# Splitting the scan's products by weight columns, half of the array each

## The chip, the cores and the metric

The kernel runs on one core of one Trainium2 chip. Its time is the device time of one execution in microseconds, and smaller is better. The core has a matrix engine (TensorE, PE in the profile, its weight loads PEld), a vector engine (VectorE, DVE), an activation engine (ScalarE, ACT), a general engine (GpSimd, POOL) and a queue that issues most transfers (SyncE, SP). Each reads its own list of instructions in order, and they wait for one another by semaphores. TensorE takes a stationary operand (the weights, loaded ahead), streams a moving operand past it, and writes the product to PSUM, where the other engines read it. The stationary operand's columns become the product's partitions.

## The reference

One layer of a bidirectional mixer on 128 context tokens and 2048 latent tokens, all in f32, with 1024 channels. The normalised and modulated input goes through one wide projection. Half of the channels are eight heads of 64 with a delta-rule recurrence, run once per direction; the other half is a short gated convolution. An output projection and a last norm follow. What the change touches is the recurrence:

```python
def step(S, inp):
    r_t, w_t, k_t, v_t, kk_t, a_t = inp
    s_kk = jnp.einsum('bdhij,bdhj->bdhi', S, kk_t)
    S = (S * w_t[..., None, :] - s_kk[..., :, None] * (kk_t * a_t)[..., None, :]
         + v_t[..., :, None] * k_t[..., None, :])
    return S, jnp.einsum('bdhij,bdhj->bdhi', S, r_t)
s_final, ys = lax.scan(step, s0.astype(f32), xs)
```

The latent scans start from cached states (`state_wkv`), the context scans from zero, and the context's final states are an output too.

## The kernel before, in words

**Phase 1** makes the projections in blocks of 384 tokens and stores the scan's operands to memory. Its products (mm..., lines 158 to 160) use the whole array. Line 188 (`mod_rows`) makes the modulation rows: weights of 32 columns, each put on another strip of 32 of the array's columns (`ps[q:q + 32, :]`).

**Phase 2** is the scan. Tokens are cut into chunks of 64. Within a chunk the recurrence is solved with matrices, so that one product takes a chunk's state to the next. The work is cut into 17 stages: each takes one pair of heads in both directions (`gi` 0 and 1) and eight chunks of each; one stage is the context's. The stages overlap. While stage s is scanned, the following ones are prepared:

- `partM` (stage s+3): psF and psG (line 829, masked by VectorE at 830) and transposes psQ (822).
- `partI` (stage s+3): GpSimd inverts small triangular matrices (lines 851 to 872, tiles ab and zt), stores the inverse, and `partW` loads it again as zc (line 896).
- `partU`, `partB` (stage s+1): psU and psW (lines 910 and 917, tiles of 32x32 of the array, two at a time on different tiles), psX (936) and psE (947). VectorE masks psE into E (line 948).
- `partS` (stage s): the scan. For a chunk, direction and head, line 987 multiplies E, 128 rows by 128 columns, as the weights, by sv, 128 rows by 64 columns. sv holds the state in its upper 64 rows and the chunk's values in its lower 64. Of the product psS, the upper 64 partitions are the next state, the lower 64 the chunk's outputs.

Line 1000 (VectorE) scales the upper half by pc into the next chunk's sv, on which that direction's next product waits. After four chunks `outputs` copies or adds the lower half to y (lines 716 and 1017). Where a new pair of heads begins, its start state comes in by line 979 (in_st) and VectorE takes its mean off in lines 981 to 983.

**Phase 3**, the output projection (lines 1219 to 1221, psa and psu), fills in towards the end of the scan and goes on after it.

What sets the order: the generators above are woven by small tables (`ORDER`, `MORD`), and then the framework schedules each engine's instructions by its own estimate of times. So an edit to one line can move instructions on all engines, SP's loads among them. SP and GpSimd issue transfers strictly in their order; a load that waits holds those behind it.

Of the kernel before, what the change touches and what calls it, by code (L numbers as in the profile page):

```python
# [627 lines left out]
def phase2(K):  # L628
    nc, tc, A, S = K.nc, K.tc, K.A, K.S
    V, G, P, T = nc.vector, nc.gpsimd, nc.scalar, nc.tensor  # L630
# [102 lines left out]
    def tl(shape, tag, b, pool=None, dt=F32):  # L733
        return (pool or O.l0).tile(shape, dt, tag=tag, name=f"{tag}_{K.u()}", bufs=b)
# [29 lines left out]
    H0, H1, FULL = slice(0, 64), slice(64, 128), slice(0, 128)  # L764
# [187 lines left out]
    def partS(s, st, nxt):  # L952

        sp = {}
        for i in range(8):
            for gi, g in enumerate(st.g):
                d = g.d
                ctx = g.blk is None
                u = i % 4 * 2 + i // 4 if ctx else i
                u = u if d == 0 else 7 - u  # L960
                p, c = g.units[u]
                if ctx:
                    first = c == (0 if d == 0 else 1)
                    lastc = not first
                else:
                    first = c == (2 if d == 0 else 33)
                    lastc = c == (33 if d == 0 else 2)
                sv = g.sv
                n, k = (u // 4 if d == 0 else 1 - u // 4), u % 4

                m, q = (u % 2, u // 2) if ctx else (u // 4, u % 4)
                if i == 0 and not ctx and gi in held:
                    G.tensor_copy(sv[0:64, u], held.pop(gi)[:])
                if first:
                    if ctx:
                        G.memset(sv[0:64, u], 0.0)
                    else:
                        x = sv[0:64, u]
                        D(x, A["st0"][:, d, 2 * p:2 * p + 2, :])
                        mn = tl([64, 2], "mn", 2)  # L980
                        V.tensor_reduce(mn[:], x, mybir.AxisListType.X, ALU.add)
                        V.tensor_scalar(mn[:], mn[:], -1.0 / 64, None, ALU.mult)
                        V.tensor_tensor(x, x, mn[:].unsqueeze(2).broadcast_to((64, 2, 64)), ALU.add)
                if i % 4 == 0:
                    sp[gi] = O.pS.tile([128, 4, 2, 64], F32, tag="S", name=f"psS{s}_{gi}_{i}")
                for hd in range(2):
                    T.matmul(sp[gi][:, q, hd, :], g.E[n][:, k, hd, :], sv[:, u, hd, :], start=True, stop=True)  # L987
                if not (lastc and not ctx):
                    if ctx and lastc:
                        so = tl([64, 2, 64], "so", 2)  # L990
                        dst = so[:]
                    elif (not ctx) and i == 7:
                        if nxt.g[gi].blk is None:
                            held[gi] = tl([64, 2, 64], "held", 2)
                            dst = held[gi][:]
                        else:
                            dst = nxt.g[gi].sv[0:64, 0 if d == 0 else 7]
                    else:
                        dst = sv[0:64, u + (1 if d == 0 else -1)]
                    r = V.tensor_tensor(dst, sp[gi][0:64, q], B.pc[0:64, d, 2 * p:2 * p + 2, c:c + 1].broadcast_to((64, 2, 64)), ALU.mult)  # L1000
                    O.scaled = r.ins
                    if ctx and lastc:
                        D(S["nst"][:, d, 2 * p:2 * p + 2, :], so[:])
                if i % 4 == 3:
                    outputs(g.units[0][0], g.blk, m, sp[gi])
            yield

    def outputs(p, blk, m, ps):

        y, there = ynew.setdefault((p, blk), (None, []))  # L1010
        if y is None:
            y = tl([128, 4, 128], "y", 5)
            ynew[p, blk] = y, there
        r = slice(m * 64, m * 64 + 64)
        src = ps[64:128].rearrange("p q h v -> p q (h v)")
        if m in there:
            V.tensor_tensor(y[r], src, y[r], ALU.add)  # L1017
        else:
            copy("o", y[r], src)
        there.append(m)  # L1020
        if len(there) == 4:
            ynew.pop((p, blk))
            pend.append(finish(p, blk, y))
# [67 lines left out]
    def main():  # L1091
# [12 lines left out]
        for s in range(NST):  # L1104
# [30 lines left out]
            for i, _ in enumerate(partS(s, st, sts.get(s + 1))):  # L1135
                for _ in range((2, 2, 2, 1, 1, 0, 0, 0)[i]):
                    next(m, None)
                next(tail, None)
                if s < NST - 1:
                    emit(i + 1)  # L1140
                for f in todo[:1] if s < NST - 3 else todo:
                    next(f, None)
# [203 lines left out]
```

## Time and profile before

| what | value |
|---|---|
| three runs | 1759.25, 1768.68, 1767.44 us, median 1767.44 |
| profiled execution, span from first to last instruction | 1770.7 us |
| TensorE busy | 1649.1 us, 93% of the span |
| VectorE, ScalarE, GpSimd busy | 65%, 47%, 34% |
| mean granted TensorE clock | 0.968 |
| psS (line 987) | 1088 instructions, from 1045.2 to 1605.2 us |

The profiled execution has no time of its own beside its span; the page gives the span only. A row of a group reads: line, engine, operation, written tile <- read tiles, shape, count, then busy time in all and mean of one in ns, then the engine's idle time just before and what ended it. A row of the order of time reads: start in us, length in us, engine, line, operation, tiles, shape, count of merged instructions, and in brackets a wait before it. Lengths of TensorE instructions overlap the next one, since they are pipelined; so what an instruction takes is read from one start to the next. A product in f32 shows as two instructions. A row of waits reads: engine, line that waited, what it waited for, us in all, times, longest.

### The profile page before, as it was taken

The page shows a single profiled execution, that of the slowest core. Times are in us where ns is not written, and L with a number is a line of the kernel's source. Part 1 is how long each engine was busy: PE and PEld are TensorE (multiplying, and loading weights), DVE is VectorE, ACT ScalarE, POOL GpSimd, SP SyncE. Part 2 cuts the span into 40 slices and gives each one's busy share as a digit, 9 for nine tenths or more (in the row PEclk, how much of TensorE's full clock was granted, in tenths as well). Part 3 has the DMA queues.
Part 4 walks back from the last instruction along what each step waited for, and adds up shares of the span by engine and source line. Part 5 has one row for each costly group of instructions (what it writes and reads, how often), then busy time and mean ns, then how long its engine had stood idle before and what let it go on. Part 6 is the DMA issues. An engine that isn't in the chain of part 4 may idle for free. (4 is left out here: it accounts for less than half of the span.)

```text
span 1770.7 us, 33010 instructions
## 1 busy us (share of the span) xinstructions
PE 1649.1 (93%) x12400; PEld 1557.3 (88%) x12400; DVE 1157.2 (65%) x2197; ACT 831.2 (47%) x1607; POOL 601.3 (34%) x1089
## 2 busy tenths in 40 slices
PE   5999899999899999999999999899899899899998
PEld 3898899899888999999999989899799899787786
DVE  5998897545777635478843466777677677556333
ACT  4565544224454312255522177667567576433222
POOL 0132210001122100022205528877767868223221
PEclk9999999999899999999999989999899899899999
DMA  9788786564788743478776376767667784645432
GB/s 363 218 244 241 231 253 244 200 237 127 167 193 184 207 153 128 152 191 218 243 249 209 127 178 170 167 178 193 158 172 197 166 193 115 177 149 192 155 129 104
DMA packets 315376, 335.16 MB, mean 189 GB/s; under 512 B 166920, under 2 KB 263560, under 8 KB 301136
## 3 DMA queue, kind: packets, MB, share of 16 engines
q1 hardware_dynamic: 242912, 323.99, 61.5%
q10 hardware_dynamic: 70944, 4.60, 3.0%
q0 software_dynamic: 1360, 4.46, 0.7%
q8 instruction: 98, 1.61, 0.4%
q14 instruction: 62, 0.51, 0.1%
HBM read 221.16 MB, written 111.82 MB: 188 GB/s over the span
## 5 line engine op out<-in xcount | busy, mean ns | idle before, releaser
L871 POOL TENSOR_TENSOR zt<-zt,ztmp 128x30 f32<-128x30 f32 (+7 forms) x510 | 201.9, 396 | 39.7
L987 PE MATMUL psS<-sv,E 128*128 128x64 f32 x1088 | 153.1, 273 | 2.7 <-DVE sv L1000 2.5
L947 PE MATMUL psE<-str,stl 128*128 128x128 f32 x1088 | 149.3, 283 | 5.6 <-ACT str L714 3.8
L987 PEld LDWEIGHTS psS<-sv,E 128*128 128x128 f32 x1088 | 143.3, 197 | 5.9 <-DVE sv L1000 4.3
L947 PEld LDWEIGHTS psE<-str,stl 128*128 128x128 f32 x1088 | 135.0, 196 | 6.9 <-ACT str L714 4.6
L868 POOL TENSOR_TENSOR ztmp<-ab,zt 128x60 f32<-128x60 f32 (+7 forms) x255 | 132.4, 519 | 19.4
L716 ACT COPY bd<-rr 64x512 f32<-64x512 f32 x136 | 83.9, 617 | 90.2 <-issue 35.1
L314 POOL TENSOR_TENSOR shk<-rawl 128x384 f32<-128x384 f32 (+1 forms) x24 | 20.1, 838 | 277.1 <-ACT rawl L310 271.3
L948 DVE TENSOR_TENSOR E<-psE,msk 128x512 f32<-128x512 f32 x136 | 93.4, 687 | 24.3 <-PE psE L947 22.2
L936 PE MATMUL psX<-F,zb 128*128 128x128 f32 x544 | 79.6, 299 | 18.4 <-DVE E L948 13.2
L1000 DVE TENSOR_TENSOR sv<-psS,pc 64x128 f32<-64x128 f32 x254 | 67.9, 277 | 37.3 <-PE psS L987 35.6
L936 PEld LDWEIGHTS psX<-F,zb 128*128 128x128 f32 x544 | 71.8, 209 | 21.7 <-DVE E L948 16.1
L158 PE MATMUL mmv<-h,w 128*128 128x384 f32 (+1 forms) x192 | 70.1, 365 | 19.2 <-ACT q1r L312 10.1
L1282 POOL TENSOR_TENSOR z<-z,x 128x512 f32<-128x512 f32 x32 | 43.7, 1367 | 129.0 <-DVE z L1278 106.8
L829 PE MATMUL psF<-rr,bd 128*128 128x128 f32 x544 | 79.7, 294 | 2.7 <-ACT bd L716 1.8
L829 PE MATMUL psG<-rr,bd 128*128 128x128 f32 x544 | 74.7, 283 | 4.8 <-DVE F L830 4.8
L829 PEld LDWEIGHTS psF<-rr,bd 128*128 128x128 f32 x544 | 71.8, 206 | 3.3 <-issue 2.9
L829 PEld LDWEIGHTS psG<-rr,bd 128*128 128x128 f32 x544 | 68.3, 198 | 5.1 <-DVE F L830 5.0
L195 POOL TENSOR_TENSOR hsls<-sq,hshs 128x384 fp32r<-128x384 f32 (+1 forms) x24 | 31.6, 1318 | 109.5 <-DMA scr_vt<-vt 36.5
L159 PE MATMUL mmv<-h,w 128*128 128x384 f32 (+1 forms) x192 | 68.5, 357 | 0.0
L160 PE MATMUL mmv<-h,w 128*128 128x384 f32 (+1 forms) x192 | 68.0, 354 | 0.1
L158 PE MATMUL mmg<-h,w 128*128 128x384 f32 (+1 forms) x192 | 63.4, 330 | 4.0 <-ACT ta L374 2.0
(308 smaller groups left out, 5193.2 us busy)
## 6 DMA issues: line engine op xcount, KB each, us to landing
w<-scr_wsp SPq DMA_DIRECT2D x68, 1024.0 KB, 6.6
scr_wsp<-w SPq DMA_DIRECT2D x34, 1024.0 KB, 5.6
rr<-scr_ops SPq DMA_DIRECT2D x64, 512.0 KB, 5.0
scr_ops<-sp SPq DMA_DIRECT2D x160, 192.0 KB, 5.1
wr<-in_win SPq DMA_DIRECT2D x34, 512.0 KB, 7.5
ab<-scr_at SPq DMA_DIRECT2D x34, 256.0 KB, 3.8
x<-in_x SPq DMA_DIRECT2D x17, 512.0 KB, 3.7
wadas<-in_wada SPq DMA_DIRECT2D x8, 1024.0 KB, 15.2
```

What stands on the lines that cost most here:

```text
L158: T.matmul(ps[:, :n], w[:, 0, k], hh[:, 0, k, :n], start=k == 0, stop=False)
L159: T.matmul(ps[:, :n], w[:, 0, k], hh[:, 1, k, :n], start=False, stop=False)
L160: T.matmul(ps[:, :n], w[:, 1, k], hh[:, 0, k, :n], start=False, stop=k == 7)
L716: (V.tensor_copy if k in ON_DVE else P.copy)(dst, src)
L829: T.matmul(ps[:, i, :].rearrange("p (a b) -> p a b", b=64), w[:, u, :], x[:, :, u, :], start=True, stop=True)
L868: G.tensor_tensor(tv, ab[:, j:j + 2, j + 2:32].unsqueeze(1).broadcast_to((128, kn, 2, n)), zt[:, :kn, j:j + 2].unsqueeze(3).broadcast_to(( ...
L871: G.tensor_tensor(zt[:, :kn, j + 2:32], zt[:, :kn, j + 2:32], tv[:, :, r], ALU.subtract)
L936: T.matmul(px[:, i, :], B.zb[:, gi, us.start + i, :], g.F[:, us.start + i, :], start=True, stop=True)
L947: T.matmul(pe[:, i, hd, :].rearrange("p (b t) -> p b t", b=2), g.lt[:, :, hd, us.start + k + i].rearrange("p b t -> p (b t)"), g.rt[:, :, ...
L948: V.tensor_tensor(g.E[n][:, k:k + 2].rearrange("p a b c -> p (a b) c"), pe[:].rearrange("p a b c -> p (a b) c"), B.msk[:, ME[g.d]].unsquee ...
L987: T.matmul(sp[gi][:, q, hd, :], g.E[n][:, k, hd, :], sv[:, u, hd, :], start=True, stop=True)
L1000: r = V.tensor_tensor(dst, sp[gi][0:64, q], B.pc[0:64, d, 2 * p:2 * p + 2, c:c + 1].broadcast_to((64, 2, 64)), ALU.mult)
```

## The change

The product of a chunk and a head is issued as two: the first with E's first 64 columns as the weights, which writes psS's upper 64 partitions (the next state), the second with E's last 64 columns, which writes the lower 64 (the outputs). Both move the same sv. H0 and H1 are the slices 0 to 64 and 64 to 128. What is computed is the same.

```diff
                 for hd in range(2):
-                    T.matmul(sp[gi][:, q, hd, :], g.E[n][:, k, hd, :], sv[:, u, hd, :], start=True, stop=True)
+                    for r in (H0, H1):
+                        T.matmul(sp[gi][r, q, hd, :], g.E[n][:, k, hd, r], sv[:, u, hd, :], start=True, stop=True)
```

Lines below 987 move down by one: what is line 1000 above is 1001 in the changed kernel, and the products are in its line 988.

The schedule changes with it. In the rows below psS_0 and psS_1 are the two directions, and the number behind x counts products or pieces. TensorE in the second half of a stage of the scan, before:

```order
L947 MATMUL psE_0_10_11520<-str_10008,stl_10002 128x128 x4
L829 MATMUL psF_1_1_11635<-rr_8836,bd_8831 128x128 x3
L987 MATMUL psS_0_0_11558<-sv_11104,E_11366 128x64 x2
L829 MATMUL psF_1_1_11635<-rr_8836,bd_8831 128x128
L829 MATMUL psG_1_0_11641<-rr_8836,bd_8832 128x128 x3
L947 MATMUL psE_1_10_11526<-str_10009,stl_10003 128x128 x4
L987 MATMUL psS_1_0_11562<-sv_11113,E_11374 128x64
L947 MATMUL psE_0_11_11532<-str_10008,stl_10002 128x128 x4
L987 MATMUL psS_1_0_11562<-sv_11113,E_11374 128x64
```

and the same place now:

```order
L947 MATMUL psE_0_10_11616<-str_10008,stl_10002 128x128 x4
L829 MATMUL psF_1_1_11743<-rr_8836,bd_8831 128x128 x2
L988 MATMUL psS_0_0_11654<-sv_11168,E_11454 64x64 x4
L829 MATMUL psF_1_1_11743<-rr_8836,bd_8831 128x128 x2
L829 MATMUL psG_1_0_11749<-rr_8836,bd_8832 128x128 x2
L988 MATMUL psS_1_0_11660<-sv_11177,E_11462 64x64
L947 MATMUL psE_1_10_11622<-str_10009,stl_10003 128x128 x4
L988 MATMUL psS_1_0_11660<-sv_11177,E_11462 64x64
L947 MATMUL psE_0_11_11628<-str_10008,stl_10002 128x128 x4
L988 MATMUL psS_1_0_11660<-sv_11177,E_11462 64x64 x2
```

Steps of four pieces stand alone between products on the full array, and some steps are cut into runs of one or two pieces, as single products were before. Elsewhere the steps of both directions follow directly on one another, eight pieces in a row:

```order
L988 MATMUL psS_0_4_10588<-sv_10024,E_10332 64x64 x4
L988 MATMUL psS_1_4_10594<-sv_10033,E_10340 64x64 x4
L917 MATMUL psW_10549<-zc_10329,bu 32x32 x32
L988 MATMUL psS_0_4_10588<-sv_10024,E_10332 64x64 x4
L988 MATMUL psS_1_4_10594<-sv_10033,E_10340 64x64 x4
L829 MATMUL psF_0_1_10838<-rr_8835,bd_8831 128x128 x4
L988 MATMUL psS_0_4_10588<-sv_10024,E_10332 64x64 x4
L988 MATMUL psS_1_4_10594<-sv_10033,E_10340 64x64 x4
L936 MATMUL psX_0_0_10617<-F_8825,zb 128x128 x4
```

psW stands between two such runs. In the whole changed order the 1088 pieces stand in 240 unbroken runs: 24 of one piece, 13 of two, 11 of three, 128 of four, 7 of five, 1 of six, 2 of seven, 52 of eight, 1 of ten and 1 of twelve. From the first psS to the last the full array is left for narrower pieces 216 times (205 for psS, 11 for psU or psW), where before it was left 47 times, for psU and psW. 35 times a run of psS comes directly behind psU or psW, and 28 times one of those directly behind psS.

SP's queue also changed. At the stage that begins the third pair of heads (sv's new tiles are loaded here, with the values from scr_vt and the start state from in_st; ab and zc belong to GpSimd's inverses), before:

```order
L851 DMA ab_13060<-scr_at 64x1024 x2
L1074 DMA scr_mixT<-yo_12978 128x512
L896 DMA zc_13137<-scr_zt 64x16x32 x2
L1038 DMA sg_13234<-scr_sg 128x512
L759 DMA sv_13126<-scr_vt 64x8x128
L979 DMA sv_13126<-in_st 64x128
L759 DMA sv_13135<-scr_vt 64x8x128
L1038 DMA w_13330<-scr_q 128x512
L979 DMA sv_13135<-in_st 64x128
L805 DMA rr_8835<-scr_ops_57 128x2x512
```

and now:

```order
L979 DMA sv_13350<-in_st 64x128
L896 DMA zc_13361<-scr_zt 64x16x32
L759 DMA sv_13359<-scr_vt 64x8x128
L896 DMA zc_13361<-scr_zt 64x16x32
L1039 DMA w_13566<-scr_q 128x512
L805 DMA rr_8835<-scr_ops_57 128x2x512
L783 DMA stl_10002<-scr_ops_57 64x4x64 x2
L780 DMA str_10008<-scr_ops_57 64x2x256
L780 DMA str_10009<-scr_ops_59 64x2x256
L783 DMA stl_10003<-scr_ops_59 64x4x64 x2
L805 DMA rr_8835<-scr_ops_57 128x2x512
L979 DMA sv_13359<-in_st 64x128
```

The first direction's start state now stands ahead of zc, and the second direction's further behind it, beyond the loads of the next block. At the stage that begins the fourth pair the two moved in the same way; at the second pair, where one start state stood ahead of zc, both now do.

## The prediction

> **What bounds the kernel now.** I read the page's first part, then a table of stretches, then who TensorE waited for, then the order of time around the scan.
>
> ```profile
> PE 1649.1 (93%) x12400; PEld 1557.3 (88%) x12400; DVE 1157.2 (65%) x2197; ACT 831.2 (47%) x1607; POOL 601.3 (34%) x1089
> L987 PE MATMUL psS<-sv,E 128*128 128x64 f32 x1088 | 153.1, 273 | 2.7 <-DVE sv L1000 2.5
> L987 PEld LDWEIGHTS psS<-sv,E 128*128 128x128 f32 x1088 | 143.3, 197 | 5.9 <-DVE sv L1000 4.3
> ```
> ```profile
> core 0: us, PE busy (x) PEld busy (x) DVE busy (x) ACT busy (x) POOL busy (x), PEclk, DMA share, GB/s
> 1045.00:1605.00 560.00, 520.50 (x5910) 499.26 (x5909) 397.26 (x837) 355.08 (x646) 375.23 (x807) 0.96 0.67 169
> ```
> ```profile
> PE psX L936 <- DVE E L948: 13.2, 14, 3.8
> PE psQ L822 <- DVE GA L830: 7.6, 1, 7.6
> PE psE L947 <- ACT str L714: 3.8, 1, 3.8
> PE psX L936 <- ACT stl L714: 3.5, 1, 3.5
> PE psS L987 <- DVE sv L1000: 2.5, 6, 0.7
> ```
>
> The edited line runs from 1045 to 1605 us, 560 us of the span. TensorE is at work in 93% of that stretch (520.5 of 560). The waits shown are its large ones there (us in all, times, longest): some 38 us with the small ones, and the scan's own dependence, psS on sv, is 2.5 of them. So the stretch hangs on TensorE's issue and the scan's latency hardly counts. What counts is how much TensorE time a psS group takes from the instruction ahead to the one behind. Mean durations of 273 ns do not say that, because instructions overlap; starts in order of time do:
>
> ```profile
> 1103.32 1.06 PE L947 MATMUL psE<-str,stl 128*128 128x128 f32 x8
> 1104.21 0.56 PE L987 MATMUL psS<-sv,E 128*128 128x64 f32 x4
> 1104.60 1.11 PE L947 MATMUL psE<-str,stl 128*128 128x128 f32 x8
> 1105.55 0.56 PE L987 MATMUL psS<-sv,E 128*128 128x64 f32 x4
> ```
>
> From 1104.21 to 1105.55 are twelve instructions in 1.34 us: 0.112 each, and psE alone the same (0.89 for eight up to 1104.21). psS moves 64 columns and psE 128, yet both take 0.112, so psS is paced by loading 128 columns of weights. A product in f32 is two instructions (544 products, x1088), so one step of one direction, four instructions, takes 0.45 us.
>
> **The change, part by part.** Each product becomes two pieces of 64 weight columns, one on each half of the array: 1088 pieces. Three things need a price: a pass of 64 columns, whether two halves run at once, and going from the whole array to halves and back. No row shows a half of 64 columns; narrower pieces show each.
>
> ```profile
> 253.42 0.34 PE L158 MATMUL mmb<-h,w 128*128 128x384 f32 x1
> 253.59 0.34 PE L159 MATMUL mmb<-h,w 128*128 128x384 f32 x1
> 253.77 0.33 PE L160 MATMUL mmb<-h,w 128*128 128x384 f32 x1
> 254.03 1.05 PE L188 MATMUL psgr<-wgate,scp 128*32 128x512 f32 x4
> 255.01 0.44 PE L158 MATMUL mmc<-h,w 128*128 128x384 f32 x1
> 255.29 0.34 PE L159 MATMUL mmc<-h,w 128*128 128x384 f32 x1
> ```
> ```profile
> 34.46 1.06 PE L188 MATMUL psrow<-wadas,scp 128*32 128x512 f32 x8
> 35.45 0.44 PE L159 MATMUL mmf<-h,w 128*128 128x384 f32 x1
> ```
>
> *At once.* Line 188 puts products of 32 weight columns on different column strips. 128 moving f32 columns took 0.112, so 512 take some 0.445. Four such instructions on two strips took 254.03 to 255.01, 0.98 us; eight on four strips took 34.46 to 35.45, 0.99. That is two passes plus 0.09: strips run side by side. I take the halves to do so as well.
>
> *Switching.* The last mmb starts at 253.77 and streams 0.17 (its neighbours' spacing), to 253.94; the strips start at 254.03: 0.09 to empty the array. On the way back another 0.09 (0.98 less two passes). Then the first mmc takes 0.28 to the next where 0.17 is usual: its load of 128 columns, 0.11, has nothing to hide behind. So leaving and returning costs 0.09+0.09+0.11 = 0.29, plus the first narrow load. The scan has such a place already:
>
> ```profile
> 1092.80 0.56 PE L987 MATMUL psS<-sv,E 128*128 128x64 f32 x4
> 1093.29 0.24 PE L917 MATMUL psW<-zc,bu 32*32 32x32 f32 x2
> 1093.46 0.66 PE L987 MATMUL psS<-sv,E 128*128 128x64 f32 x4
> 1094.05 1.19 PE L917 MATMUL psW<-zc,bu 32*32 32x32 f32 x62
> 1095.17 1.10 PE L987 MATMUL psS<-sv,E 128*128 128x64 f32 x8
> ```
>
> From 1093.29 to 1094.05, 0.76 us hold four psS (0.45), two tiny passes (0.06) and one return and one leaving: 0.25, near 0.29. The Trainium skill, TensorEngine Tiling (Array Packing), Key Properties, says that changing the tiling mode, not merely the tile, drains the engine. It has no price; these 0.09s agree. Without it the sum below would fall by some 36 us, to 22 less than before.
>
> *A pass.* The 62 psW instructions and one return take 1.12 us (1094.05 to 1095.17). Less 0.09 that is 0.033 for each two (two tiles at once) at 32 columns, against 0.112 at 128; on the line between, 64 columns take 0.059. Bounds: 0.056, half of 0.112, if nothing in it is fixed; 0.112 if the width gains nothing. I take 0.059, since 32 columns scale almost in proportion.
>
> *The sum* needs the order. The changed order has the 1088 pieces in 240 unbroken runs: 24 of one piece, 13 of two, 11 of three, 128 of four (one step), 7 of five, 52 of eight (both directions), and one each or two of 6, 7, 10 and 12. A run of four needs four passes of each half, a run of eight eight, one or two pieces two: 1132 in all. The full array is left 216 times (205 for psS, 11 for psU and psW), before 47 times. 63 changes go straight between psS's halves and psU's or psW's small tiles.
>
> - Streams: 1132 x 0.059 = 67, less 1088 x 0.112 = 122: **-55 us**.
> - Leaving and returning: (216-47) x 0.29 = 49; 63 x 0.09 = 6; the first narrow load of 240 runs x 0.06 = 14: **+69 us**.
> - Together **+14 us** of TensorE. A lone step costs 0.59 instead of 0.45, a run of eight 0.83 instead of 0.90: four out of five runs lose.
>
> Bounds: with a pass of 0.056, +11; of 0.112, +74; halves that don't overlap at all, 2176 passes of 0.059, +76; a drain of nothing, -22.
>
> *What lies beside it.* VectorE's reads of psS by line 1000, ScalarE's copies and the stored bytes stay as they are. Of TensorE's waits the 14 for E come mostly right behind a psS group (L948 late by 13.2 us); the added 0.14 falls into each of these: -2 us.
>
> *What the order moves.* SP's queue is read in order, and it has shifted past a wait:
>
> ```profile
> 1256.82 0.54 SPq L1074 DMA_DIRECT2D scr_mixT<-yo  x1
> 1263.03 1.34 SPq L896 DMA_DIRECT2D zc<-scr_zt  x2
> 1264.41 0.66 SPq L1038 DMA_DIRECT2D sg<-scr_sg  x1
> 1265.16 0.59 SPq L759 DMA_DIRECT2D sv<-scr_vt  x1
> 1265.80 0.63 SPq L979 DMA_DIRECT2D sv<-in_st  x1
> ```
> ```profile
> 1269.84 0.28 DVE L981 TENSOR_REDUCE mn<-sv 64x2 f32<-64x128 f32 x1 [8.07 <-DMA sv<-in_st]
> DVE mn L981 <- DMA sv<-in_st: 14.7, 4, 8.1
> ```
>
> SP sits from 1257.4 to 1263.0 at the load of zc, which needs GpSimd's stored inverse. Behind it stands the start state (in_st) of a new head pair, which VectorE needs at line 981; VectorE then stood 8.07 us and TensorE 7.6 (psQ, above). A second such place, shown by the row of four waits together, makes psX's longest wait for E, 3.8 us. In the changed order the first direction's start state is loaded ahead of zc, at both places: 7.6 + 3.8 = 11 us to gain at most. But the second direction's now stands behind the next block's loads, and VectorE's line 981 for it ahead of an E: nothing to gain at least. Middle: -5.
>
> 14 - 2 - 5 = **+7 us** on the profiled execution: 1770.7 to 1778. Its span lies 3.3 above the median of the runs, 1767.4, so on the median **1774**, with its own range 1764 to 1786.
>
> **The rivals.**
> 1. *The waits swallow it: faster, some 1752.* If stages hang on SP's and GpSimd's chain (zc, in_st) rather than on issue, the 14 vanish in 38 us of waits and the start states give their 11 back. The clock helps:
> ```profile
> 1265.70:1276.00 10.30, 4.44 (x19) 4.04 (x20) 5.91 (x15) 2.68 (x5) 8.91 (x18) 0.50 1.03 251
> ```
> ```profile
> 1271.37 1.11 PE L822 MATMUL psQ<-idt,rr 128*128 128x128 f32 x4 [7.63 <-DVE GA L830]
> ```
> The granted clock falls to 0.50 during the wait and stays there until 1276; the 4.6 us of work from 1271.4 on lose 2, and with the second place some 4. 1767 - 11 - 4 = 1752. For it: SP's wait; against it: TensorE at work 93%. Chance 0.2.
> 2. *The second start state stalls: slower, some 1788.* Between zc and its load stand nine others of some 0.6 us each in the rows above, some of which wait for TensorE. If it lands later than VectorE comes to it, line 981 holds VectorE and E comes late. At two places 9 us each (six of loads, three of that wait) replace 7.6 and 3.8: +7, and 14 with nothing hidden, 1767 + 21. Against it: VectorE has some fifteen more instructions ahead of that line than before. Chance 0.17.
> 3. *Halves take turns:* if a product's pieces don't overlap, +76: 1843. Against it the strips of line 188. Chance 0.05.
> 4. *Halves at no price: much faster.* The same page of the Trainium skill, Theoretical Speedup, gives up to 2x for a small dimension of 64 or less. As a mechanism here: psS's 122 us become 67 and the drains hide: 1767 - 55 = 1712. The 0.09s and the bare 0.11 load speak against it. Chance 0.03.
>
> **How the numbers follow.** The forecast has 0.55. The measurement tells 0.5% (9 us) from no change: slower starts at 1776, faster at 1758. Of the forecast's 0.55, 0.32 lie within and 0.23 above; rival 1 gives 0.17 to faster and 0.03 to the same, rival 2 0.14 to slower and 0.03 to the same, rival 3 0.05 to slower, rival 4 0.03 to faster. Faster 0.20, same 0.38, slower 0.42. The range, 1752 to 1794, reaches to rivals 1 and 2 and leaves out 3 and 4 and half a tail.
>
> **What would show it.** A run of four psS pieces should start 0.20 behind the last full-array instruction, and the next full-array start should come 0.4 later, bare by 0.11; starts of the two halves a few ns apart show them side by side. The line-188 pattern failing at 64 columns (passes of 0.11, halves in turn) makes me wrong upwards; psS starting with no gap, downwards. Line 981's waits of 14.7 us should fall below 10. TensorE's instructions rise by 1088; if its summed waits fall by more than 15 us, the order decided and not the array.

## The result, and the profile after the change

The changed kernel takes 1776.88 us (median of 6 runs, 1773.62 to 1781.74) beside 1768.06 us for the kernel before in the same comparison: ratio 1.0055, 95% interval [1.0033, 1.0077]. It is some 9 us slower, and the interval lies on both sides of the half per cent that the prediction had as its bound for "slower". The forecast was 1774. The profiled execution has a span of 1776.1 us, 5.4 more than before.

The page's first part, and the rows of the edited line on TensorE and its weight loads (busy time, mean ns of one, idle time ahead):

```profile
PE 1658.7 (93%) x13488; PEld 1525.6 (86%) x13488; DVE 1162.5 (65%) x2197; ACT 832.0 (47%) x1607; POOL 598.8 (34%) x1089
L988 PE MATMUL psS<-sv,E 128*64 128x64 f32 x2176 | 121.3, 236 | 4.1 <-DVE sv L1001 4.1
L988 PEld LDWEIGHTS psS<-sv,E 128*64 128x64 f32 x2176 | 87.5, 140 | 35.3 <-issue 6.0
```

TensorE has the 1088 instructions more that were expected. Line 988 is busy 32 us less than before (121.3 against 153.1), and yet TensorE as a whole is busy 10 us more. A line's busy time overlaps that of its neighbours, so these rows don't say where the time went. The weight loads of the narrow pieces have 35.3 us of idle time ahead of them, against 5.9 before, and the starts show what it is.

Starts in order of time, in the changed kernel, at the place of which the prediction quoted the rows of before (start, time to the end of the last, engine, line, operation, count):

```profile
1099.22 1.16 PE L829 MATMUL psF<-rr,bd 128*128 128x128 f32 x8
1100.31 0.69 PE L988 MATMUL psS<-sv,E 128*64 128x64 f32 x16
1100.92 2.05 PE L936 MATMUL psX<-F,zb 128*128 128x128 f32 x16
1102.90 0.45 PE L988 MATMUL psS<-sv,E 128*64 128x64 f32 x8
...
1106.96 1.06 PE L947 MATMUL psE<-str,stl 128*128 128x128 f32 x8
1107.95 0.45 PE L988 MATMUL psS<-sv,E 128*64 128x64 f32 x8
1108.33 1.16 PE L947 MATMUL psE<-str,stl 128*128 128x128 f32 x8
1109.42 0.45 PE L988 MATMUL psS<-sv,E 128*64 128x64 f32 x8
```

An x8 on line 988 is a lone step now, four pieces of two instructions each. From one lone step to the next, with eight psE between, it is 1.47 us (1107.95 to 1109.42); before it was 1.34 (1104.21 to 1105.55). So a lone step costs 0.13 us more, where the prediction had 0.59 against 0.45. The psE behind it take 1.09 (1108.33 to 1109.42) where the eight ahead of it take 0.99 (1106.96 to 1107.95): 0.10 is a weight load that nothing covers (a bare load), and 0.09 in each is the array running empty, ahead of the pieces or behind them. An x16 is two steps together: 0.61 to the next instruction (1100.31 to 1100.92), and 1.98 for sixteen psX, which is 0.19 more than sixteen times 0.112. Together 0.80, where eight whole instructions take 0.90.

Who TensorE waited for in the stretch of the scan, changed kernel (us in all, times, longest), and two of VectorE's waits in it:

```profile
PE psX L936 <- DVE E L948: 13.6, 14, 2.1
PE psS L988 <- DVE sv L1001: 4.1, 6, 1.5
PE psE L947 <- DVE E L948: 3.4, 3, 1.6
PE psE L947 <- ACT stl L714: 2.9, 3, 1.3
PE psQ L822 <- DVE GA L830: 2.4, 1, 2.4
```
```profile
DVE mn L981 <- DMA sv<-in_st: 10.9, 5, 3.6
DVE zr L902 <- DMA zc<-scr_zt: 7.2, 3, 4.0
```

psQ's long wait fell from 7.6 to 2.4 and psX's longest for E from 3.8 to 2.1, as the prediction's bound of 11 us supposed. But the sum of all rows of this view is 34.9 us (1045 to 1650 us) against 39.1 before: only 4 less. VectorE waits 10.9 instead of 14.7 for the start state, and 7.2 for zc, which stands in the same queue and cost this before:

```profile
DVE zr L902 <- DMA zc<-scr_zt: 1.6, 2, 1.2
```

### The profile page after: what moved, and what is told of

It is laid out like the page before. It is cut to its first block, busy times and chain, and to the rows that moved or that the text cites. A ratio compares the mean times of both kernels' runs of the same rounds, so it can differ in the third digit from the quotient of the medians.

```text
span 1776.1 us, 35182 instructions
## 1 busy us (share of the span) xinstructions
PE 1658.7 (93%) x13488; PEld 1525.6 (86%) x13488; DVE 1162.5 (65%) x2197; ACT 832.0 (47%) x1607; POOL 598.8 (34%) x1089
## 5 line engine op out<-in xcount | busy, mean ns | idle before, releaser
L988 PE MATMUL psS<-sv,E 128*64 128x64 f32 x2176 | 121.3, 236 | 4.1 <-DVE sv L1001 4.1
L988 PEld LDWEIGHTS psS<-sv,E 128*64 128x64 f32 x2176 | 87.5, 140 | 35.3 <-issue 6.0
L936 PE MATMUL psX<-F,zb 128*128 128x128 f32 x544 | 78.5, 297 | 15.3 <-DVE E L948 13.6
L1001 DVE TENSOR_TENSOR sv<-psS,pc 64x128 f32<-64x128 f32 x254 | 67.5, 277 | 38.3 <-PE psS L988 35.2
L829 PE MATMUL psF<-rr,bd 128*128 128x128 f32 x544 | 85.4, 299 | 4.2 <-ACT bd L716 2.0
L158 PE MATMUL mmv<-h,w 128*128 128x384 f32 (+1 forms) x192 | 68.1, 355 | 17.3 <-ACT q1r L312 10.3
L830 DVE TENSOR_TENSOR F<-psF,msk 128x512 f32<-128x512 f32 x68 | 46.4, 683 | 32.4 <-PE psF L829 17.9
L159 PE MATMUL mmv<-h,w 128*128 128x384 f32 (+1 forms) x192 | 66.3, 345 | 0.0
```

What stands on the lines that cost most here:

```text
L158: T.matmul(ps[:, :n], w[:, 0, k], hh[:, 0, k, :n], start=k == 0, stop=False)
L159: T.matmul(ps[:, :n], w[:, 0, k], hh[:, 1, k, :n], start=False, stop=False)
L829: T.matmul(ps[:, i, :].rearrange("p (a b) -> p a b", b=64), w[:, u, :], x[:, :, u, :], start=True, stop=True)
L936: T.matmul(px[:, i, :], B.zb[:, gi, us.start + i, :], g.F[:, us.start + i, :], start=True, stop=True)
L988: T.matmul(sp[gi][r, q, hd, :], g.E[n][:, k, hd, r], sv[:, u, hd, :], start=True, stop=True)
```

## The experiments

In several of these kernels each engine's order is fixed, so that the array and the order can be told apart. A list from a built kernel gives the order, and each instruction gets a dependency on the one ahead of it that makes no semaphore (shortened):

```python
for s in steps:                      # positions, from the other kernel's built order
    at += s
    for i in units[at]:              # a pair of pieces is one unit
        if prev is not None:
            tc.add_manual_dep(i, prev.name, mybir.DependencyInfo(NoSync, DATA), reason="order")
        prev = i
```

All ratios are to the kernel before, run beside. "By the prices" in the expectations means the prediction's prices with that kernel's own counts.

**Split pieces, old order.** The changed line 988, with every engine in the order of the kernel before.

> The split products of the change, but every engine's instructions held in the order of the kernel before (a pair of pieces stands where its product stood). Theory (the array's price): the 1088 pieces stand in 218 runs with 1088 passes, the full array is left 210 times (47 before), 55 changes between narrow tiles: streams 1088 x 0.059 - 122 = -58, switching 163 x 0.29 + 55 x 0.09 + 218 x 0.06 = +65, together +7 us of TensorE, a little of it hidden: +5 us, 1773. Line 981 should wait as before, some 14.7 us. Rival (the order decides): 0. Rival (switching has no price): -50.

1779.68 us, ratio 1.0074 [1.0053, 1.0096]: +13 us (9 to 17). The array's price is there without any change of order, and neither rival holds. But it is 8 more than the +5 expected. In its trace TensorE's waits come to 45.1 us, 6 more than before, with one of 8.8 (psX for E) and one of 8.2 (psE for str). The span is 9.0 longer: 6 are these waits, and the other 3 passed ahead of the first psS (it starts at 1048.4 instead of 1045.3), where nothing was changed. So this one trace doesn't show the 7 us that the prices give TensorE.

**Whole products, new order.** The other way round: line 987 as it was, every engine in the order of the changed kernel.

> The whole products of the kernel before, but every engine's instructions held in the order of the changed kernel. Theory: what the order gives is what line 981 and the load of zc no longer cost, -5 us (0 to -11), TensorE at work as before: 1763. The changed kernel should then be 14 us or more slower than this one, all of it TensorE's (streams -55, switching (229-39) x 0.29 + 50 x 0.09 + 240 x 0.06 = +74: +19, some of it hidden). Rival (the order, and not the array, made the changed kernel slower): this one is slower than before by the same 9 us.

1770.60 us, ratio 1.0003 [0.9981, 1.0025]: nothing, where -5 was expected. The order neither slows nor speeds the kernel by more than some 4 us. VectorE's two waits in this kernel, and three of TensorE's, show why the gain did not come:

```profile
DVE mn L981 <- DMA sv<-in_st: 13.6, 6, 4.0
DVE zr L902 <- DMA zc<-scr_zt: 5.7, 3, 2.7
```
```profile
PE psS L987 <- DVE sv L1000: 6.5, 8, 2.0
PE psE L947 <- ACT stl L714: 5.5, 3, 2.5
PE psQ L822 <- DVE GA L830: 3.4, 2, 2.4
```

The wait of 8.1 at one place has become six of up to 4.0: nearly the same sum (13.6 against 14.7), and 4 us more for zc. On TensorE psQ's wait is 4 us shorter, but psS waits 4 us more for sv, and there are new waits for stl: in all 38.3 against 39.1. In this same order the changed kernel is 0.52% slower (1.0055 against 1.0003), some 9 us (4 to 15): that is the split alone. By the prices it is +19 of TensorE, so about half arrives.

**Switching alone.** The kernel before with a tiny narrow product ahead of each step, which the step overwrites:

```diff
+                T.matmul(sp[gi][H0, q, 0, 0:2], g.E[n][:, k, 0, H0], sv[:, u, 0, 0:2], start=True, stop=True)
                 for hd in range(2):
                     T.matmul(sp[gi][:, q, hd, :], g.E[n][:, k, hd, :], sv[:, u, hd, :], start=True, stop=True)
```

> The kernel before, with one narrow product more (64 weight columns, 2 moving columns) ahead of every scan step; the step then overwrites what it wrote. Nothing is saved, so it prices the switching by itself: the full array is left 289 times (47 before): 242 x 0.29 = 70, 18 narrow changes 2, first narrow loads 272 x 0.06 = 16, the added instructions 544 x 0.059 = 32: +120 us of TensorE, less what falls into waits, 1870 to 1887. Rival (switching has no price): +32, 1800. Rival (TensorE's issue is not the bound): under +15.

1813.27 us, ratio 1.028 [1.0247, 1.0313]: +50 us (44 to 55). Switching does have a price, and TensorE's issue is the bound, but the forecast of more than 100 is far off. The trace tells where it went. First the price, by starts in order of time:

```profile
1102.63 1.06 PE L829 MATMUL psF<-rr,bd 128*128 128x128 f32 x8
1103.61 0.28 PE L986 MATMUL psS<-sv,E 128*64 128x2 f32 x2
1103.82 0.66 PE L988 MATMUL psS<-sv,E 128*128 128x64 f32 x4
1104.41 0.28 PE L986 MATMUL psS<-sv,E 128*64 128x2 f32 x2
```

Eight psF take 0.98 up to the narrow ones (0.89 and 0.09 to empty the array); two narrow ones take 0.21; the four whole ones behind take 0.59, that is 0.45, 0.09 of emptying and 0.05 of a bare load. So a switch with its two instructions costs 0.35 here, not 0.44; the bare load behind them is shorter than the 0.10 behind the pieces of 64 moving columns. 272 of them make 95 us. The span grew by 51.8. The rest was in the waits, which are these four rows in the whole stretch:

```profile
PE psX L936 <- DVE E L948: 1.1, 2, 0.6
PE psE L947 <- DVE E L948: 1.1, 2, 0.9
PE psE L947 <- ACT str L714: 0.7, 1, 0.7
PE psX L936 <- ACT zb L714: 0.4, 1, 0.4
```

39.1 us of waits fell to 3.3. So 36 us of the added TensorE work went where TensorE had waited, and of what came on top of it, some 59, the greater part arrived (52 in the span, 50 by the ratio).

**Pairs.** The changed kernel with both directions' steps kept together: the first direction's piece is placed behind the second's last scaling and its E, and the pieces go ahead of other ready work (shortened).

```diff
                     for r in (H0, H1):
-                        T.matmul(sp[gi][r, q, hd, :], ...)
+                        with tc.high_priority():
+                            m_ = T.matmul(sp[gi][r, q, hd, :], ...)
+                        if gi == 0 and hd == 0:
+                            # NoSync dependencies of m_ on the other direction's E and on its last scaling
```

> The changed kernel with the pieces of both directions' steps kept together more often: a step of the first direction is placed behind the other direction's last scaling and its E, and the pieces go ahead of other ready work. 181 runs (90 of four, 91 of eight), 1088 passes, full array left 143 times, 129 narrow changes. Theory: streams -58, switching 96 x 0.29 + 129 x 0.09 + 181 x 0.06 = +51: -7 us of TensorE against before and -23 against the changed kernel; the first direction then waits for the second, some us more of psS waits: 1755 to 1768. Rival (price per piece and not per switch): as the changed kernel, 1777. Rival (order decides): either side, with waits and not instruction counts that differ.

1775.18 us, ratio 1.0044 [1.0022, 1.0066]: as slow as the changed kernel, though the price per switch says 23 us of TensorE less. The work did fall: the span is 1.1 above that of before and the waits are 45.2, 6.1 more, so TensorE's own work is 5 less (7 by the prices). What it saved it now waits for:

```profile
PE psX L939 <- DVE E L951: 9.6, 12, 1.5
PE psX L939 <- ACT zb L715: 7.7, 13, 1.3
PE psG L830 <- DVE GA L831: 6.5, 3, 2.5
PE psE L950 <- ACT stl L715: 6.2, 5, 2.6
```

Before, ScalarE's zb held psX once, for 1.3 us; now thirteen times. That the pieces' priority pushed back the work that others wait for fits these rows; no run shows it by itself.

**Split where it should pay.** Old order on every engine. Only those 138 of the 272 steps are split that stand in runs of two steps or more, or next to psU or psW, where the array is narrow already (the edit against the line of the changed kernel; FULL is the whole slice, and a step not in SPLIT stays whole):

```diff
-                    for r in (H0, H1):
+                    for r in ((H0, H1) if ST.step in SPLIT else (FULL,)):
```

> The order of the kernel before on every engine; only those scan steps are split that stand in runs of two steps or more, or next to the narrow products psU or psW (138 of 272). Theory: 552 passes, full array left 73 times (47 before), 55 narrow changes, 81 runs: streams 552 x 0.059 - 552 x 0.112 = -29, switching 26 x 0.29 + 55 x 0.09 + 81 x 0.06 = +17: -12 us of TensorE. If all of it reaches the end 1756; since waits took 6 us back in the run with pairs, 0 to -12, middle -6: 1762. Rival (every split product costs, some 13 us for 544): +6. Rival (nothing that TensorE saves reaches the end): 0.

1767.40 us, ratio 0.9991 [0.9971, 1.0012]: not told apart from before, and below the +6 of a price per product. In the trace the span is 7.0 shorter, and the waits are 47.9 us, 8.8 more:

```profile
PE psX L936 <- DVE E L948: 19.4, 17, 7.9
PE psE L947 <- ACT str L714: 8.8, 4, 7.5
PE psQ L822 <- DVE GA L830: 5.0, 1, 5.0
```

Three of the 7 us passed ahead of the first psS (1042.3 instead of 1045.3). From there on TensorE's work fell by 13 (12 by the prices), and 9 of that turned into waits.

**Split where it should not pay.** The same order, and the other 134 steps split.

> The other half of the same: the order of the kernel before, and only the 134 steps split that stand alone between instructions of the whole array (131 runs of four pieces, 6 of two). Theory: streams 536 x (0.059 - 0.112) = -28, switching 137 x 0.29 + 137 x 0.06 = +48: +20 us of TensorE, less a third that falls into waits: +13, 1781. Rival (a price per split product): +6. The two halves together should come to what the split in the old order gave, +13.

1773.52 us, ratio 1.0033 [1.0014, 1.0052]: +6 us (2 to 9), where +13 was expected. That is what a price per split product would give, but the run with the other half of the steps has excluded that one. The rows are those of the kernel before that the prediction quoted (psE, psS, psE, psS), the work between them the same:

```profile
1107.19 1.06 PE L947 MATMUL psE<-str,stl 128*128 128x128 f32 x8
1108.17 0.45 PE L988 MATMUL psS<-sv,E 128*64 128x64 f32 x8
1108.55 1.16 PE L947 MATMUL psE<-str,stl 128*128 128x128 f32 x8
1109.64 0.45 PE L988 MATMUL psS<-sv,E 128*64 128x64 f32 x8
```

From psE to the second psS it is 2.45 us against 2.23 before. Yet the waits fall from 39.1 to 31.8. The same 131 lone steps, taken from the records of single instructions from the last one ahead to the third one behind, have a median of 0.91 us against 0.78 before (+0.13), and a mean, without cases over 3 us, of 0.99 against 0.93 (+0.06). So on the mean less than half of the price lengthens these places, which fits switches that lie where TensorE would have waited.

The halves of the selection give -2 and +6, but the whole of it in the same order +13. With intervals of about 4 us on each, the 9 us between are more than chance would make likely; why both together cost more than their sum stays open.

**One direction only.**

```diff
-                    for r in (H0, H1):
+                    for r in ((H0, H1) if gi == 0 else (FULL,)):
```

> The changed kernel with only the first direction's products split, the second's whole as before; the order falls as it falls. Half as many pieces, but 171 runs, of 1 to 8, full array left 191 times, 19 narrow changes, 600 passes. Theory: streams 600 x 0.059 - 544 x 0.112 = -26, switching 144 x 0.29 + 19 x 0.09 + 171 x 0.06 = +54: +28 us of TensorE, more than when both are split (+16), some two thirds of it at the end: +14 to +20, 1785. Rival (a price per piece): +5, 1773.

1776.19 us, ratio 1.0046 [1.0026, 1.0066]: +8 us (5 to 12). Half of the pieces cost as much as all of them. A price per piece would give +5, which is within the interval, so it is not excluded by this run alone; the forecast of +14 to +20 is. The waits fell here by 9.5 (29.6 against 39.1).

**The same half twice in a row.**

```diff
-                for hd in range(2):
-                    for r in (H0, H1):
+                for r in (H0, H1):
+                    for hd in range(2):
                         T.matmul(sp[gi][r, q, hd, :], ...)
```

> The changed kernel with the four pieces of a step in another order: both heads' states (first half of the array) and then both heads' outputs (second half). 234 runs, full array left 224 times. Theory if each half takes its pieces independently: as the changed kernel, 1777. If pieces start in program order, and one that finds its half at work holds those behind it (in the run with pairs one place with the same half twice in a row cost 0.05 us): a lone step takes 0.12 us more and a run of eight 0.12 to 0.23, +22 to +27 us of TensorE, 1790 to 1800.

1782.67 us, ratio 1.0075 [1.0044, 1.0106]: the interval overlaps that of the changed kernel, and lies nearer to it than to the 22 us or more of TensorE's work that pieces holding each other would cost. The starts decide:

```profile
1101.23 0.46 PE L988 MATMUL psS<-sv,E 128*64 128x64 f32 x8
1101.62 0.49 PE L829 MATMUL psF<-rr,bd 128*128 128x128 f32 x2
...
1105.31 0.73 PE L988 MATMUL psS<-sv,E 128*64 128x64 f32 x16
1105.97 2.05 PE L936 MATMUL psX<-F,zb 128*128 128x128 f32 x16
```

A lone step takes 0.39 against 0.38, a run of two steps 0.66 against 0.61. So the second half's pieces do not stand behind the first half's; only in longer runs is one pass lost.

**The selection in the other orders.** The same rule (split where two steps stand together or next to psU or psW), in the order of the changed kernel and in that of the run with pairs.

> The order of the changed kernel on every engine; only those steps are split that stand in runs of two steps or more, or next to psU or psW (137 of 272); the others whole. By the prices: 548 passes, full array left 75 times (39 for whole products in this order), 46 narrow changes, 82 runs: streams 548 x (0.059 - 0.112) = -29, switching 36 x 0.29 + 46 x 0.09 + 82 x 0.05 = +19: -10 us of TensorE. The whole products in this order took as long as the kernel before; in the old order the same selection saved TensorE some 15 us and the end 2. Theory (what TensorE saves turns into waits for E): 1764 to 1768. Rival (this order has shorter waits, so the saving gets through): 1757 to 1760.

> The order of the run with pairs on every engine, split only where two steps stand together or next to psU or psW (236 of 272 steps; 91 runs of eight, 54 of four), the four pieces of a step alternating between the halves throughout. By the prices: 944 passes, full array left 107 times (47 before), 129 narrow changes, 145 runs: streams 944 x (0.059 - 0.112) = -50, switching 60 x 0.29 + 129 x 0.09 + 145 x 0.05 = +36: -14 us of TensorE, 9 less than the run with pairs (1775). Theory (the end follows TensorE only where no other wait is near; pairs wait for E and for ScalarE's copies): 1768 to 1773. Rival (the end follows TensorE): 1754. Rival (the pairs' order itself costs 10 us or more): 1773 to 1776.

1766.54 us, ratio 0.9987 [0.9966, 1.0008], and 1770.44 us, ratio 1.0021 [0.9999, 1.0043]. Both lie where the theory put them: the first -2 us for a TensorE saving of 10, the second +4 for one of 14. But that the saving turns into waits is not what the first trace shows. Its waits are 40.3 us, 38.3 with whole products in the same order. From the first psS to the end it takes 713.2 us against 720.6, so 7 of the 10 came through there; the first psS starts 6 us later (1053.2 against 1047.1), behind the same TensorE instructions. Whether that was chance, or the scan then begins with more done ahead, one trace can't tell. With pairs, psX waits the same 7.7 us in thirteen places for ScalarE's zb, whatever is split. That points to the pairs' order as what costs; whole products in that order were not run.

**The start state taken out of the queue.** Whole products and the old order; all start states are loaded once, ahead of the stage (shortened).

```diff
+        B.st0 = cp.tile([128, 8, 64], F32, name="st0")
+        for d in range(2):
+            D(B.st0[d * 64:d * 64 + 64], A["st0"][:, d])
...
-                        x = sv[0:64, u]
-                        D(x, A["st0"][:, d, 2 * p:2 * p + 2, :])
+                        h = slice(d * 64, d * 64 + 64)
+                        x = B.st0[h, 2 * p:2 * p + 2, :]
...
-                        V.tensor_tensor(x, x, mn[:]. ...)
+                        V.tensor_tensor(sv[0:64, u], x, mn[h]. ...)
```

> Whole products and the order of the kernel before on every engine; the one difference: all start states are loaded once, ahead of the stage, into a tile of their own, and line 981 reads that instead of a load that stands behind zc in SP's queue (eight loads less there; the same three VectorE instructions). Theory of the prediction's step on the order: line 981's 14.7 us of waits go to 0, and with them what TensorE stood for them, 7.6 (psQ) + 3.8 (psX's longest): -11 us at most, -5 in the middle, 1757 to 1763. Rival (the next wait on the same chain, zc's load behind GpSimd's inverse at line 902, takes their place): 0, and zr's waits for zc rise from 1.6 to some 10.

1761.90 us, ratio 0.9953 [0.9933, 0.9973]: -8 us (5 to 12), inside the bound of 11. Line 981 has no wait any more, and what VectorE waits for zc is hardly longer than before (1.6):

```profile
DVE zr L905 <- DMA zc<-scr_zt: 2.0, 1, 2.0
```
```profile
PE psX L939 <- DVE E L951: 9.3, 12, 2.6
PE psE L950 <- ACT str L717: 8.8, 4, 4.0
PE psQ L825 <- DVE GA L833: 0.5, 1, 0.5
```

psQ's 7.6 are 0.5, psX's longest wait for E 2.6 instead of 3.8. A part came back as waits for str (3.8 before, 8.8 now).

**Both.** The early start state, and the split where it should pay.

> The same with the split where two steps stand together or next to psU or psW (138 of 272 steps), in the order of the kernel before. That split by itself saved TensorE some 15 us in the trace and the end 2, with TensorE's waits 9 us longer, the long ones (7.9 for E, 7.5 for str, 5.0 for GA) where VectorE stood 17.6 us for the start state. Theory (the saving was lost at the start state): without that wait some 10 of the 15 get through beside what the run with whole products gains: 1748 to 1756. Rival (other waits are as near): within 3 us of the run with whole products and early states.

1757.28 us, ratio 0.9943 [0.9921, 0.9965], the shortest of all: 10 us below before. But beside the run with whole products it is 2 to 5 us (0.1% by the ratios, 4.6 by the medians), within both intervals: the saving itself is not told apart from nothing. The theory that the split's saving had been lost at the start state alone, 1748 to 1756, asked for some 10, which is more than the two intervals leave (7):

```profile
PE psX L939 <- DVE E L951: 15.3, 15, 3.3
PE psE L950 <- ACT str L717: 5.5, 3, 4.0
PE psW L920 <- ACT bu L719: 3.4, 7, 0.8
```

psX waits 15.3 us for E instead of 9.3, and the waits in all are 36.2 instead of 33.2: other waits are near.

## Why the prediction was right, and where it was right by luck

The total was right: 1774 forecast, 1776.88 measured, inside its own range, and "slower" had the largest chance. Its steps fared differently, and that they added up is luck.

**Pass and overlap: right.** In the records of single instructions of a lone step the two halves start at 205 and 212 ns behind the last full-array start, then at 311 and 318, and after that every 58 ns. Halves run side by side, a pass is 0.058 (0.059 forecast), and only the first is longer, by 0.05 (0.06 forecast). The rows of line 188 carried over from 32 columns to 64, and rival 3, halves in turn, is out.

**Switching: right.** 0.09 to empty the array, 0.09 back, 0.10 of bare load. A lone step costs 0.13 more (0.14 forecast), a run of two steps 0.10 less (0.07 forecast). That the array empties at a change of mode is what the Trainium skill says in TensorEngine Tiling (Array Packing), Key Properties; these rows agree and give the price. Rival 4, no price for switching, is out, since the split in the old order is slower and not 50 us faster.

**The count: slightly wrong.** My counts took the psT rows for part of the scan. The full array is left 229 times and not 216, and 50 changes and not 63 are between narrow tiles. By the prices the sum is +17, not +14.

**What waits hide: wrong.** I took 2 us, since only the 14 waits for E seemed to stand right behind a psS group. In the same order the split cost 9 us of the 19 priced; the 272 added switches left 3.3 of 39.1 us of waits; the lone steps paid on the mean 0.06 of 0.13. So a third to a half of an added price arrived: 9 of 19, 6 of 20 (split where it should not pay), 8 of 28 (one direction). The split in the old order is the exception, 13 for a price of 7. Of savings hardly anything arrived: -12 by the prices made -2 (split where it pays), -10 made -2, and -14 made +4, the last in another order. In the traces with 272 switches, and with the split where it pays, the missing part stands in TensorE's waits; for the others the waits are not its measure.

**What the order moves: wrong.** -5 was forecast, and the whole products in the new order came out at 0. The rows from which the bound was made were right: with the load really out of the queue 8 of the 11 us came. The error is in the step from "the first direction's start state is loaded ahead of zc" to a gain. The other direction's still stands in the queue, the sum of line 981's waits stayed (13.6), and zr waited for zc instead.

So two wrong terms replaced each other, by luck: 2 hidden and 5 won in the forecast, some 8 to 10 hidden and nothing won in the runs. The forecast for the profiled execution was 1778, and it was 1776.1.

**Of the signs that were named,** the start 0.20 behind (0.205), the next full start 0.4 later (0.38), the bare load (0.10), the few ns between halves (7) and the 1088 instructions came out. Line 981 below 10 us did not (10.9). TensorE's waits fell by 4, not by more than 15, so by that sign it was not the order that decided.

**Rival 1** named a real mechanism, waits that swallow, and its size was too large: part of the price went, not all, and the start states gave nothing back in this order. **Rival 2**, a second start state that stalls, did not happen: the longest wait at line 981 is 3.6.

What stays open: how much of a price arrives, and why the split in the old order costs 13 us for a price of 7. Work here is the span less TensorE's waits in one execution, and that is a rough reading: between the kernel before and the one with the early start state it differs by 10, though they do the same products. Two reasons show in the record. Ahead of the first psS these kernels issue the same TensorE work (5812 to 5814 instructions), and yet that psS starts anywhere from 1040.8 to 1053.2 us. And the profiled execution of the kernel before was a long one: an execution's time is its span and 1.8 us wherever both are on record, so its 1770.7 stands for 1772.5, some 4 above the median of 1768. The differences of spans given above are too small by about that much, which is about the gap between the 9.0 and the 13 of the split in the old order.

The granted clock is too small a rival for what is hidden. Among executions of the kernel before, one with a clock higher by 0.01 was 3 to 8 us shorter. The mean clock of the executions was 0.968 to 0.969 for the kernel before, 0.971 for the changed kernel, and within 0.002 of the kernel before, run beside, for both runs that swap the order and for the two partial splits in the old order and the one in the new. It lay further off, upwards, in the run with one direction (0.974 against 0.968) and the two with pairs (0.972 and 0.973), where it can hide 1 to 4 us of the price.

## What to carry to other kernels

A narrow tile on a part of the array saved time nearly in proportion to its columns here (0.058 for 64 against 0.112 for 128), but each run of narrow instructions between full ones paid some 0.33 us; count the runs in the built order before counting the products, and expect nothing from splitting but where the run is long or the array is narrow already, and little even there (-2 us, not told apart from nothing). An engine at work in 93% of a stretch isn't a bound that passes on every microsecond: of additions of some 20 us to its work a third to a half arrived, of savings of some 10 next to nothing, while of a large addition most arrived once the waits were used up. A load in a queue that is read in order is best taken out of that queue; an order that merely moves it past one wait hands it to the next.

## What was not expected

- Pieces of one half in a row hardly cost anything: in a lone step the second half's first piece still started 13 ns behind the first half's first (7 ns when the halves alternate), and the next full-array instruction came 0.39 instead of 0.38 us later. Two pieces of the same half that stand ahead do not hold the other half's.
- The way back from narrow to full was cheaper behind products of two moving columns: 0.05 us of bare load, against 0.10 behind those of 64.
- 36 us of added work in 560 went into waits, in a stretch where TensorE seemed the only bound.
